# Delta-rule chain on block-diagonal 128x128 weights, modulation products in quarters, in a two-layer hybrid diffusion step

## The chip, the cores and the metric

The kernel runs on one core of a Trainium2 chip. The metric is the device time of one execution in microseconds (us), given as the median of several runs. TensorE is called PE in the rows, its weight load PEld; VectorE is DVE, ScalarE is ACT, GpSimd is POOL, and SP is the queue of SyncE, which issues the DMAs.

## The reference

One inference step of a backbone with two layers, on 128 context and 512 latent tokens of width 1024. Each layer has a mixer block with three branches (latent attention; gated linear attention; gated DeltaNet), whose results are projected, gated, summed and projected again, and then a SwiGLU block. Shift, scale and gate of both blocks come from a modulation. What the change touches is this:

```python
# modulation, per layer: six vectors of 1024 for the latent tokens, six for the context
mod = silu(cond) @ w_mod[l] + b_mod[l]
sh_a, sc_a, g_a, sh_f, sc_f, g_f = split(mod, 6)
...
h = h + g_a * y
...
# gated DeltaNet, 8 heads of 64, chunks of 64 tokens, both directions
def step(s, inp):
    u_n, w_n, qd_n, ke_n, a_n, ge_n = inp
    v_new = u_n - w_n @ s
    o_n = qd_n @ s + a_n @ v_new
    s = ge_n[..., None, None] * s + ke_n.T @ v_new
    return s, o_n
```

`u_n` and `w_n` are solutions of a triangular system of the chunk. All values are float32.

## The kernel before, in words

**Layout and large products.** Activations lie with channels on the 128 partitions and all 640 tokens in the free dimension. The large products (input projection, branch projections, output projection, SwiGLU) are one fixed sequence, an object `G` of class `Stream`. A weight tile of 128x512 is loaded (`wr`), rounded by ScalarE into `wh` (L465), and the rest is formed by GpSimd as `wl` (L466); each has three buffers. The activations are split in the same way (`xh`, `xl`; `oh`, `ol` for the branches). A block of 128x128 weights then gives six matmuls of 320 columns on L474: high by high, high by low, low by high, for two halves of the tokens. The result lies in a PSUM tile `gm` of the tag `g`, which has three buffers. When an output tile is done, a function posted for it reads it, such as `h_update` (L637), the residual update of the mixer's output projection `wo0` to `wo7`.

**Order.** Between the steps of the branches the program calls `fill(name)`, which emits as many steps of `G` as a table of numbers (`FILL`) gives for that place. A scheduler then orders the instructions of each engine by priorities and data; what stands in a queue at the end is fixed, and each engine works its queue in order. All the DMAs that are spoken of here are issued by SP, one after the other, and a DMA into a buffer that is still read waits there with all DMAs behind it.

**The chain.** `gdn_chain` (L924) works on one pair of heads `p` (four pairs per layer), on 10 chunks and in two directions: direction 0 runs forward, direction 1 backward. In a pair the two heads take the partitions 0 to 63 and 64 to 127. `steps` does one step of both directions:

- `k` times state (`ch<-S,bd_k`), then on VectorE `cy_` = that times a scale plus `v` (L947);
- `cy_` through the solved triangular matrix `t0` or `t1` (`ch<-cy_,bd_t`), then on VectorE the scaled copy `vs` (L959) and on ScalarE two copies to `VN` (L962), kept for the output;
- `kt` times `vs` (`ch<-vs,bd_kt`), and on VectorE the state's update (L973).

Each of these three products is done by `mm_heads` as two matmuls, with 64x64 weights and 64 columns, one per head. A layer has 224 such head pairs of products. Behind the steps of a pair come the output products: `pqs` (L996) with `bd_q`, whose 128x128 weights hold both heads on the diagonal and zeros elsewhere, and `pas` (L1001), then a norm and 128x128 transposes. `chain_load` loads the weights of the next pair, and the zeros of `bd_q` are written once per layer by two memsets (L1710).

**The modulation products.** In layer 0, the 20 rows 16 to 35 of the modulation weights, 16 to 23 of which are the mixer's gate, are multiplied beside the chain by `ModVe(bd, 4, 2)`: VectorE multiplies a weight tile `wmt` with the condition `cbb` and sums it up (L549, one step for latent and one for context, each with a read of the accumulator). The 1024 products of a row are split in two halves of 512 columns, `wmt` has four buffers, and a step is put behind every chain step; what is left over follows behind the chains in program order. Then the halves are summed (L555), and `mod_fix` adds the bias and scales the gate (L564, L570), which `h_update` reads. The rest of the rows is done later by steps of 1024 columns.

Of the kernel before, what the change touches and what calls it, by code (L numbers as in the profile page):

```python
# [9 lines left out]
F32 = mybir.dt.float32  # L10
# [8 lines left out]
P = 128  # L19
# [6 lines left out]
NCH = T // 64  # L26
# [257 lines left out]
class Stream:  # L284
    """Matrix products in a fixed order, emitted piece by piece between other work."""

# [86 lines left out]
def tile_hybrid(ctx: ExitStack, tc, a):  # L373
# [126 lines left out]

    # ---- modulation
    def mod_load(f, pool_):
# [19 lines left out]
    class ModVe:  # L522
        """Products of the condition with rows of the modulation weights, in single steps of the vector engine."""

# [57 lines left out]

    # ---- residual, norms
    HS = (slice(0, HF), slice(HF, T))
# [70 lines left out]
    def join(name, hs, nm, after, pre=None):  # L655
        """The last residual tile, the norm and its use, by halves of the tokens."""
        if pre:
            pre()
        G.to(name + "/0")
        G.steps(5)  # L660
        nm.fin(0)
        G.to(name)
        after(0, range(4))
        nm.fin(1)
        after(0, range(4, 8))
        after(1, range(8))

    # ---- DRAM scratch
    NB = [dp.tile([4, 2, NCH, 64, 64], F32, name=f"NB{d}") for d in range(2)]
# [6 lines left out]

    # ---- gated DeltaNet
    def gdn_gates(prm, misc, gp, X, fill):
# [141 lines left out]
    def turn_pairs(src, dst, scale):  # L820
        """Both heads of a pair from channels to tokens, chunk by chunk."""
        pv = psg("pvt").rearrange("p a (j c) -> p (a j) c", c=P)
        for j in range(5):
            pe.transpose(pv[:, j], src[:, j * P:(j + 1) * P], ident)
        for r in range(2):
            for h in range(2):
                se.activation(dst[h * 64:(h + 1) * 64, r::2], pv[r * 64:(r + 1) * 64, 0:5, h * 64:(h + 1) * 64], AF.Copy,
                              scale=scale)
# [6 lines left out]
    def gdn_solve(lp):  # L835
        Bb = lp.tile([P, 10, P], F32, name="Bb")
        ge.memset(Bb, 0.0)
        for d in range(2):
# [26 lines left out]
            for f in range(2):  # L865
                ln = slice(40 * f, 40 * f + 40)
                Lt = lp.tile([P, 10, 32], F32, name="Lt", tag="Lt")
                Rt = lp.tile([P, 10, 32], F32, name="Rt", tag="Rt")
                dma(Lt, LS[d][ln].rearrange("(g q) s c -> (q s) g c", q=4))
                for q in range(4):  # L870
                    qs = slice(32 * q, 32 * q + 32)
                    lq = slice(40 * f + q, 40 * f + 40, 4)
                    dma(Rt[qs], T3[lq, hi, hi].rearrange("g s c -> s g c"))
                    dma(Bb[qs, :, qs], N3[lq, lo, hi].rearrange("g s c -> s g c"))
                for _ in range(5):
                    yield
                def narrow(w):
                    """Bb[:, g].T @ w[:, g] for all g, by the narrow operand and a turn."""
                    pw = psb([P, 3, P], "pw")
                    for g in range(10):  # L880
                        r = slice(32 * (g % 4), 32 * (g % 4) + 32)
                        pe.matmul(pw[r, g // 4], w[:, g], Bb[:, g], start=True, stop=True)
                    wt = lp.tile([P, 3, P], F32, name="wt", tag="st")
                    se.activation(wt[:, 0:2], pw[:, 0:2], AF.Copy)
                    se.activation(wt[0:64, 2], pw[0:64, 2], AF.Copy)
                    yield
                    pt = psb([P, 3, P], "pt")
                    for i, n in ((0, P), (1, P), (2, 64)):
                        pe.transpose(pt[:, i, :n], wt[:n, i], ident[:n, :n])
                    return pt.rearrange("p i (r c) -> p (i r) c", c=32)[:, 0:10]  # L890

                pw = yield from narrow(Lt)
                for q in range(4):
                    qs = slice(32 * q, 32 * q + 32)
                    se.activation(Bb[qs, :, qs], pw[qs], AF.Copy)
                yield
                px = yield from narrow(Rt)
                xs = lp.tile([P, 10, 32], F32, name="xs", tag="Lt")
                se.activation(xs, px, AF.Copy)
                for q in range(4):  # L900
                    dma(T3[40 * f + q:40 * f + 40:4, lo, hi].rearrange("g s c -> s g c"), xs[32 * q:32 * q + 32])
                yield

    def chain_load(p, B, names):
        for n in names:
            if n in ("k", "kt"):
                dma(B[n], SPL[n][p])
                continue
            for h in range(2):
                hh = slice(h * 64, (h + 1) * 64)  # L910
                if n == "a":
                    for d in range(2):
                        dma(B[n][d * 64:(d + 1) * 64, h], SPL[f"a{d}"][p, hh])
                elif n == "q":
                    dma(B[n][hh, :, hh], SPL[n][p, hh])
                else:
                    dma(B[n][hh], TB[int(n[1])][p, h].rearrange("n s c -> s n c"))

    def mm_heads(out, w, x):
        for h in range(2):  # L920
            hh = slice(h * 64, (h + 1) * 64)
            pe.matmul(out[hh], w[hh], x[hh], start=True, stop=True)

    def gdn_chain(l, p, SC, B, kp, z, fill, mstep):  # L924
# [10 lines left out]
        def steps(sts):  # L935
            pss = [psb([P, 3, 64], "ch") for _ in sts]
            ys = []
            for (d, n, zero, dst), ps in zip(sts, pss):
                if not zero:
                    mm_heads(ps[:, 0], B["k"][:, n], S[:, n, d])  # L940
            for (d, n, zero, dst), ps in zip(sts, pss):
# [10 lines left out]
            for (d, n, zero, dst), ps, y in zip(sts, pss, ys):  # L952
                mm_heads(ps[:, 1], B[f"t{d}"][:, n], y)
            vss = []
# [11 lines left out]
            if vss:  # L966
                for (d, n, zero, dst), ps, vs in zip(sts, pss, vss):
                    mm_heads(ps[:, 2], B["kt"][:, n], vs)
                for (d, n, zero, dst), ps, vs in zip(sts, pss, vss):
# [58 lines left out]

    # ---- latent attention
    def latents(l, prm, misc, M, pj, gg, fill):  # L1030
# [223 lines left out]

    # ---- gated linear attention
    def gla(l, prm, misc, gp, oh, ol, gmf, gmb, fill, tick):
# [182 lines left out]

    # ---- the order of the large products  # L1440
    pieces = []
# [95 lines left out]

    # ---- the layers
    hctx = pool("hp0", "right")
# [35 lines left out]
    for l in range(L):  # L1575
# [107 lines left out]
        with pool("gt", "right", 2) as gt:  # L1683
# [11 lines left out]
            with pool("zs", "left") as zs:  # L1695
# [6 lines left out]
                with pool("bd", "left") as bd, pool("kp", "left") as kp:  # L1702
                    bufs = {}
                    bufs["a"] = bd.tile([P, 2, NCH, 64], F32, name="bd_a")
                    for n in ("t0", "t1", "k", "kt"):
                        bufs[n] = bd.tile([P, NCH, 64], F32, name="bd_" + n)
                    bufs["q"] = bd.tile([P, NCH, P], F32, name="bd_q")
                    mst = ModVe(bd, 4, 2).steps(0, range(16, 16 + OPT["mc"])) if l == 0 else iter(())
                    for h in range(2):
                        ge.memset(bufs["q"][h * 64:(h + 1) * 64, :, (1 - h) * 64:(2 - h) * 64], 0.0)  # L1710
                    chain_load(0, bufs, ("t0", "t1", "k", "kt"))
# [132 lines left out]
```

## Time and profile before

| | |
|---|---|
| median of 3 runs | 2895.55 us (2894.88 to 2895.70) |
| span of the profiled execution | 2896.0 us |
| PE busy | 2721.4 us (94%), 19444 instructions |
| PEld busy | 2498.5 us (86%) |
| DVE busy | 1542.6 us (53%) |
| ACT busy | 1209.0 us (42%) |
| POOL busy | 1196.0 us (41%) |
| DMA | 317.10 MB, mean 109 GB/s |
| L474 (three groups with `xh`, `xl`) | 846.2, 826.8, 832.5 us |
| L549 (all forms) | 298.6 us, 200 instructions |

Busy times can overlap: a matmul's record reaches from its start to its modelled end, so that records of neighbouring matmuls overlap, and the distance from start to start tells what one costs. A row of the timeline gathers neighbouring instructions of one kind (`x8`) and gives the start of the first and the time to the end of the last. Brackets at a row's end give the idle time ahead of it and who ended it.

### The profile page before, as it was taken

What the parts mean: (1) busy time and instruction counts of PE and PEld (TensorE: products, weight loads), DVE (VectorE), ACT (ScalarE), POOL (GpSimd) and SP (SyncE); (2) the same over time, 40 slices, a digit from 0 to 9 for tenths busy, and PEclk for the clock granted to TensorE, in tenths of its full rate; (3) what the DMA queues carried; (4) which work ended last, traced back from release to release, by engine and by line L of the source; (5) the groups of instructions that cost most, each with busy time, mean ns of one, the idle gap of its engine ahead of it and who ended that gap; (6) DMA issues with size and microseconds to landing.
All of it is one profiled execution on the core that took longest, in us unless ns stands there. A gap on an engine that the chain in (4) does not pass through costs nothing. (4 is left out here: it accounts for less than half of the span.)

```text
span 2896.0 us, 49763 instructions
## 1 busy us (share of the span) xinstructions
PE 2721.4 (94%) x19444; PEld 2498.5 (86%) x19444; DVE 1542.6 (53%) x2834; ACT 1209.0 (42%) x2276; POOL 1196.0 (41%) x872
## 2 busy tenths in 40 slices
PE   7899999889999999999998899987999999999998
PEld 4788888778779899999988888876877898999998
DVE  4765584747655699177358576556334334211212
ACT  5575655543333522122366645554333344222223
POOL 3543222333325467366445323233333264443443
PEclk9999999999999999999999999998999999999999
DMA  6254433245433355344323534332423231222222
GB/s 207 90 161 141 91 82 94 88 130 168 140 101 127 108 189 177 86 139 156 105 84 110 177 90 97 72 93 73 137 79 88 73 111 59 77 73 78 73 74 83
DMA packets 291834, 317.10 MB, mean 109 GB/s; under 512 B 163696, under 2 KB 174768, under 8 KB 291472
## 3 DMA queue, kind: packets, MB, share of 16 engines
q1 hardware_dynamic: 291600, 313.92, 37.3%
q8 instruction: 154, 2.52, 0.4%
q14 instruction: 80, 0.66, 0.1%
HBM read 266.01 MB, written 47.82 MB: 108 GB/s over the span
## 5 line engine op out<-in xcount | busy, mean ns | idle before, releaser
L466 POOL TENSOR_TENSOR wl<-wr,wh 128x512 fp32r<-128x512 f32 (+1 forms) x576 | 813.9, 1416 | 1307.0 <-ACT wh L465 1177.0
L474 PE MATMUL gm<-xh,wh 128*128 128x320 f32 x3456 | 846.2, 322 | 25.1 <-ACT xh L624 9.4
L474 PE MATMUL gm<-xh,wl 128*128 128x320 f32 x3456 | 826.8, 316 | 13.4 <-POOL wl L466 13.4
L474 PE MATMUL gm<-xl,wh 128*128 128x320 f32 x3456 | 832.5, 317 | 7.2 <-DVE xl L631 4.2
L465 ACT ACTIVATE wh<-wr 128x512 fp32r<-128x512 f32 (+1 forms) x576 | 357.6, 623 | 944.0 <-PE gm L474 648.9
L474 PEld LDWEIGHTS gm<-xh,wh 128*128 128x128 f32 x3456 | 589.6, 192 | 52.5 <-ACT xh L624 14.5
L474 PEld LDWEIGHTS gm<-xl,wh 128*128 128x128 f32 x3456 | 594.3, 192 | 25.0 <-DVE xl L631 9.8
L474 PEld LDWEIGHTS gm<-xh,wl 128*128 128x128 f32 x3456 | 592.6, 192 | 21.7 <-POOL wl L466 15.5
L549 DVE CUSTOM_DVE_ANT_0 ctb<-wmt,cbb 128x1024 f32<-128x1024 f32 (+1 forms) x200 | 298.6, 1493 | 3.4
L637 DVE SCALAR_TENSOR_TENSOR h<-gm,mod,h 128x128 f32<-128x128 f32 x144 | 55.7, 462 | 272.2 <-PE gm L474 266.1
L474 PE MATMUL gm<-ah,wh 128*128 128x320 f32 x704 | 164.6, 310 | 0.5 <-DVE h L637 0.5
L474 PE MATMUL gm<-ah,wl 128*128 128x320 f32 x704 | 164.1, 309 | 0.0
L474 PE MATMUL gm<-al,wh 128*128 128x320 f32 x704 | 163.9, 309 | 0.0
L962 ACT ACTIVATE VN<-ch 64x64 f32<-64x64 f32 x320 | 70.0, 219 | 178.5 <-DVE vs L959 164.5
L474 PEld LDWEIGHTS gm<-ah,wh 128*128 128x128 f32 x704 | 118.7, 188 | 1.6 <-DVE h L637 1.5
L474 PEld LDWEIGHTS gm<-al,wh 128*128 128x128 f32 x704 | 118.5, 188 | 0.2
L474 PEld LDWEIGHTS gm<-ah,wl 128*128 128x128 f32 x704 | 118.5, 188 | 0.0
L1773 DVE TENSOR_TENSOR th<-th,gm 128x640 f32<-128x640 f32 x44 | 36.2, 822 | 149.2 <-PE gm L474 148.4
L1766 DVE SCALAR_TENSOR_TENSOR th<-th,gm 128x640 f32<-128x640 f32 x44 | 35.9, 816 | 138.3 <-ACT th L1765 138.3
L479 POOL TENSOR_TENSOR al<-th,ah 128x640 fp32r<-128x640 f32 x44 | 89.5, 2033 | 28.0 <-DVE ah L478 28.0
L474 PE MATMUL gm<-ol,wh 128*128 128x320 f32 x384 | 99.3, 332 | 1.5 <-POOL ol L479 1.5
L474 PE MATMUL gm<-oh,wh 128*128 128x320 f32 x384 | 98.7, 334 | 0.5 <-DVE gth L1524 0.3
(747 smaller groups left out, 3822.8 us busy)
## 6 DMA issues: line engine op xcount, KB each, us to landing
wr<-in_wall_dram SPq DMA_DIRECT2D x432, 256.0 KB, 3.0
wmt<-in_wmodt_dram SPq DMA_DIRECT2D x60, 512.0 KB, 3.7
wr<-in_wfo_dram SPq DMA_DIRECT2D x64, 256.0 KB, 2.6
wr<-in_wbr_dram SPq DMA_DIRECT2D x48, 256.0 KB, 2.7
wmt<-in_wmodt_dram SPq DMA_DIRECT2D x40, 256.0 KB, 3.2
wm<-in_wmod_dram SPq DMA_DIRECT2D x16, 512.0 KB, 8.3
wr<-in_wfo_dram SPq DMA_DIRECT2D x32, 192.0 KB, 2.4
h<-in_xt_dram SPq DMA_DIRECT2D x16, 320.0 KB, 5.5
```

The source lines that it names most:

```text
L465: se.activation(wh[:, :w], wr[:, :w], AF.Copy)
L466: ge.tensor_tensor(wl[:, :w], wr[:, :w], wh[:, :w], op=ALU.subtract)
L474: pe.matmul(ps[:, c, :HF], w_[:, wsl], x_[kx][:, c * HF:(c + 1) * HF], start=(start and i == 0), stop=(stop and i == 2))
L479: (lo or ge).tensor_tensor(dst_l, src, dst_h, op=ALU.subtract)
L549: ins = ve.tensor_tensor_reduce(self.t, wm, self.c[:, i], 0.5, 0.0, ALU.mult, ALU.add, accum_out=acc[h][:, m - m0, i:i + 1])
L637: ve.scalar_tensor_tensor(hs[d][:, s:e], ps[:, c, s - c * HF:e - c * HF], g[:, d, i:i + 1], hs[d][:, s:e], op0=ALU.mult, op1=ALU.add)
L962: se.activation(VN[d * 64:(d + 1) * 64, h, n], ps[h * 64:(h + 1) * 64, 1], AF.Copy)
L1766: ve.scalar_tensor_tensor(v3(th), v3(th), 1.0, ps, op0=ALU.add, op1=ALU.mult)
L1773: ve.tensor_tensor(v3(th), v3(th), ps, op=ALU.mult)
```

## The change

The weights of the three chain products become block-diagonal 128x128, as `bd_q` has been: `t0`, `t1`, `kt` and `k` get 128 columns per chunk, each head's 64x64 block is loaded onto the diagonal, and the rest is zeroed once per layer by two memsets per buffer (ten memsets instead of two). One matmul of 64 columns then serves both heads, and `mm_heads` goes. `k` and `kt` are loaded in two DMAs of 64 partitions each instead of one of 128. `ModVe` is made with two buffers and four quarters: steps of 256 columns. Further lines of the diff only remove comments, which shifts line numbers by 8 behind the chain.

```diff
 def chain_load(p, B, names):
     for n in names:
-            if n in ("k", "kt"):
-                dma(B[n], SPL[n][p])
-                continue
             for h in range(2):
                 hh = slice(h * 64, (h + 1) * 64)
                 if n == "a":
...
-                elif n == "q":
+                elif n in ("q", "k", "kt"):
                     dma(B[n][hh, :, hh], SPL[n][p, hh])
                 else:
-                    dma(B[n][hh], TB[int(n[1])][p, h].rearrange("n s c -> s n c"))
-
-    def mm_heads(out, w, x):
-        for h in range(2):
-            hh = slice(h * 64, (h + 1) * 64)
-            pe.matmul(out[hh], w[hh], x[hh], start=True, stop=True)
+                    dma(B[n][hh, :, hh], TB[int(n[1])][p, h].rearrange("n s c -> s n c"))
...
-                    mm_heads(ps[:, 0], B["k"][:, n], S[:, n, d])
+                    pe.matmul(ps[:, 0], B["k"][:, n], S[:, n, d], start=True, stop=True)
...
-                mm_heads(ps[:, 1], B[f"t{d}"][:, n], y)
+                pe.matmul(ps[:, 1], B[f"t{d}"][:, n], y, start=True, stop=True)
...
-                    mm_heads(ps[:, 2], B["kt"][:, n], vs)
+                    pe.matmul(ps[:, 2], B["kt"][:, n], vs, start=True, stop=True)
...
-                    for n in ("t0", "t1", "k", "kt"):
-                        bufs[n] = bd.tile([P, NCH, 64], F32, name="bd_" + n)
-                    bufs["q"] = bd.tile([P, NCH, P], F32, name="bd_q")
-                    mst = ModVe(bd, 4, 2).steps(0, range(16, 16 + OPT["mc"])) if l == 0 else iter(())
-                    for h in range(2):
-                        ge.memset(bufs["q"][h * 64:(h + 1) * 64, :, (1 - h) * 64:(2 - h) * 64], 0.0)
+                    for n in ("t0", "t1", "kt", "k", "q"):
+                        bufs[n] = bd.tile([P, NCH, P], F32, name="bd_" + n)
+                    mst = ModVe(bd, 2, 4).steps(0, range(16, 16 + OPT["mc"])) if l == 0 else iter(())
+                    for n in ("t0", "t1", "kt", "k", "q"):
+                        for h in range(2):
+                            ge.memset(bufs[n][h * 64:(h + 1) * 64, :, (1 - h) * 64:(2 - h) * 64], 0.0)
```

What the scheduler makes of it is seen in three places. The first is TensorE in the chain of layer 1, before, with two matmuls (x2) per head pair:

```order
L922 MATMUL ch<-vs,bd_kt 64x64 x2
L474 MATMUL gm<-xh,wl 128x320
L922 MATMUL ch<-vs,bd_kt 64x64 x2
L474 MATMUL gm<-xh,wh 128x320 x2
L922 MATMUL ch<-S,bd_k 64x64 x2
L474 MATMUL gm<-xl,wh 128x320
L922 MATMUL ch<-S,bd_k 64x64 x2
L474 MATMUL gm<-xl,wh 128x320
L474 MATMUL gm<-xh,wl 128x320 x2
L922 MATMUL ch<-cy__21764,bd_t_20741 64x64 x2
```

and a stretch of the same chain in the changed kernel:

```order
L474 MATMUL gm<-xl,wh 128x320
L474 MATMUL gm<-xh,wl 128x320 x2
L474 MATMUL gm<-xh,wh 128x320 x2
L960 MATMUL ch<-vs,bd_kt 128x64
L932 MATMUL ch<-S,bd_k 128x64
L474 MATMUL gm<-xl,wh 128x320 x2
L474 MATMUL gm<-xh,wl 128x320
L932 MATMUL ch<-S,bd_k 128x64
L474 MATMUL gm<-xh,wl 128x320
L945 MATMUL ch<-cy__22786,bd_t_20707 128x64
```

Each `x2` has become one matmul, and chain products still stand singly or in twos between stream matmuls.

The second is VectorE at the last modulation steps of layer 0. Before, they stand in the output of the third pair of heads (`co`, `css`, L1008 to L1016), ahead of the chain of the fourth:

```order
L549 ISA ctb,macc_6408<-wmt,cbb 128x512
L549 ISA macc_6408 128x1
L555 TENSOR_TENSOR mod_102<-mod_102,macc_6408 128x40
L1012 TENSOR_REDUCE css<-co_8298 128x10
L564 TENSOR_TENSOR mod_102<-mod_102,prm_162 128x16 x2
L570 TENSOR_SCALAR mod_102<-mod_102 128x16
L1016 TENSOR_TENSOR co<-co,css 128x640
```

In the changed kernel the last ones stand right ahead of the residual updates of `wo0` to `wo2` (`h_9475` to `h_9477`), behind 30 more of their kind:

```order
L549 ISA ctb,macc_6416<-wmt,cbb 128x256
L549 ISA macc_6416 128x1
L549 ISA ctb,macc_6416<-wmt,cbb 128x256
L549 ISA macc_6416 128x1
L555 TENSOR_TENSOR mod_102<-mod_102,macc_6416 128x40
L564 TENSOR_TENSOR mod_102<-mod_102,prm_162 128x16 x2
L570 TENSOR_SCALAR mod_102<-mod_102 128x16
L637 SCALAR_TENSOR_TENSOR h_9475<-gm,mod_102,h_9475 128x128
L637 SCALAR_TENSOR_TENSOR h_9475<-gm,mod_102,h_9475 128x192
L637 SCALAR_TENSOR_TENSOR h_9475<-gm,mod_102,h_9475 128x320
L637 SCALAR_TENSOR_TENSOR h_9476<-gm,mod_102,h_9476 128x128
```

The modulation's end has moved behind all four chains and the merge of the third branch.

The third is the queue of SP where it loads the projection weights of the third branch (`wr<-in_wbr_dram`), before:

```order
L389 DMA wr<-in_wall_dram 128x512
L389 DMA wr<-in_wbr_dram 128x512 x7
L389 DMA wr<-in_wall_dram 128x512 x5
L389 DMA cbb<-in_condb_dram 128x2048
L389 DMA h_9509<-in_xt_dram 128x640
```

and in the changed kernel:

```order
L389 DMA wr<-in_wbr_dram 128x512
L389 DMA wmt<-in_wmodt_dram 128x256 x8
L389 DMA wr<-in_wbr_dram 128x512
L389 DMA wmt<-in_wmodt_dram 128x256 x2
L389 DMA wr<-in_wbr_dram 128x512
L389 DMA wmt<-in_wmodt_dram 128x256 x3
L389 DMA wr<-in_wbr_dram 128x512 x2
L389 DMA wmt<-in_wmodt_dram 128x256 x3
L389 DMA wr<-in_wall_dram 128x512
```

Loads of modulation weights now stand between the loads of the stream.

## Rows read from the trace of the kernel before

**Rows 1.** Windows: busy us (instructions) per engine, clock, DMA share; chains of layers 0, 1.

```profile
644.20:875.70 231.50, 228.06 (x1935) 182.16 (x1936) 149.70 (x454) 80.35 (x229) 74.70 (x59) 0.99 0.48 137
2079.50:2303.00 223.50, 219.92 (x1912) 176.91 (x1913) 85.78 (x286) 77.61 (x223) 69.58 (x59) 0.98 0.32 88
```

**Rows 2.** Windows, the same stretches, line L474 alone (PE, PEld).

```profile
644.20:875.70 231.50, 166.13 (x825) 124.69 (x825) 0.99 0.48 137
2079.50:2303.00 223.50, 165.14 (x816) 123.00 (x816) 0.98 0.32 88
```

**Rows 3.** Timeline of PE from 695 us: start, duration, engine, line, operation, tiles.

```profile
695.06 0.46 PE L474 MATMUL gm<-xl,wh 128*128 128x320 f32 x2
...
695.64 0.46 PE L474 MATMUL gm<-xh,wh 128*128 128x320 f32 x2
```

**Rows 4.** Windows, both chains together, line L1001 (`pas`) alone.

```profile
sum 455.00, PE 9.51 PEld 8.07; mean PE 4.75 PEld 4.04
```

**Rows 5.** Timeline of PE, chain of layer 0, around one isolated product.

```profile
712.77 0.31 PE L474 MATMUL gm<-oh,wl 128*128 128x320 f32 x1
713.01 0.33 PE L922 MATMUL ch<-vs,bd_kt 64*64 64x64 f32 x4
713.27 0.41 PE L474 MATMUL gm<-oh,wl 128*128 128x320 f32 x1
713.52 0.31 PE L474 MATMUL gm<-oh,wh 128*128 128x320 f32 x1
```

**Rows 6.** Timeline of PE, chain of layer 1, first and next `k` products of a step.

```profile
2278.26 0.45 PE L922 MATMUL ch<-S,bd_k 64*64 64x64 f32 x8
...
2282.72 0.45 PE L922 MATMUL ch<-S,bd_k 64*64 64x64 f32 x8
```

**Rows 7.** Timeline of PE, start of the kernel.

```profile
20.76 1.05 PE L519 MATMUL pmt<-C_base,mr 128*128 128x2 f32 x8 [0.80 <-DVE mr L516]
```

**Rows 8.** Timeline of PE, other 128x128 weights within the stream.

```profile
603.08 0.46 PE L474 MATMUL gm<-xh,wl 128*128 128x320 f32 x2
603.37 0.60 PE L1370 MATMUL pu<-gvt,ez 128*128 128x128 f32 x4
...
604.11 0.31 PE L474 MATMUL gm<-xl,wh 128*128 128x320 f32 x1
```

**Rows 9.** Timelines of PE, DVE and ACT, one step of pair 3, layer 0.

```profile
851.59 0.33 PE L922 MATMUL ch<-S,bd_k 64*64 64x64 f32 x4
...
852.94 0.33 PE L922 MATMUL ch<-cy__8669,bd_t 64*64 64x64 f32 x4
...
854.59 0.33 PE L922 MATMUL ch<-vs,bd_kt 64*64 64x64 f32 x4
...
855.94 0.33 PE L922 MATMUL ch<-S,bd_k 64*64 64x64 f32 x4
...
851.97 0.29 DVE L947 SCALAR_TENSOR_TENSOR cy__8669<-ch,SC,cvt 128x64 f32<-128x64 f32 x1 [0.41 <-PE ch L922]
...
855.02 0.28 DVE L973 SCALAR_TENSOR_TENSOR S<-S,GE,ch 128x64 f32<-128x64 f32 x1 [0.81 <-PE ch L922]
...
853.64 0.45 ACT L962 ACTIVATE VN<-ch 64x64 f32<-64x64 f32 x2 [3.44 <-DVE vs L959]
```

**Rows 10.** Groups by line, DVE, 640 to 880 us: busy us, mean ns | idle.

```profile
L549 DVE CUSTOM_DVE_ANT_0 ctb<-wmt,cbb 128x512 f32<-128x512 f32 x80 | 69.1, 864 | 0.3
```

**Rows 11.** Timeline of DVE: last modulation read; residual update of the second output tile.

```profile
826.02 0.08 DVE L549 DVE_READ_ACCUMULATOR2_ANT macc<- 128x1 f32 x1
...
929.72 1.13 DVE L637 SCALAR_TENSOR_TENSOR h<-gm,mod,h 128x128 f32<-128x128 f32 x3 [3.16 <-PE gm L474]
```

**Rows 12.** Tile `wmt`, its loads on SP: ns min/median/max, first and last start.

```profile
L389 SPq DMA_DIRECT2D wmt<-in_wmodt_dram x100: 327/328/1861, 641.7 to 1368.3; - x100
```

**Rows 13.** DMA issues, 600 to 940 us: KB each, median us to landing.

```profile
wmt<-in_wmodt_dram SPq DMA_DIRECT2D x40, 256.0 KB, 3.2
```

**Rows 14.** Tile `bd_q`, its memsets on POOL: ns min/median/max.

```profile
L1710 POOL MEMSET bd_q<- x4: 626/626/626, 623.4 to 2059.6; 64x640 f32 x4
```

## The prediction, made before the changed kernel ran

> **What bounds the kernel now.** The change touches two stretches, the delta-rule chains of layer 0 (644 to 876 us) and of layer 1 (2080 to 2303 us), so I read these first, by engine: TensorE is busy 228.06 of 231.50 us and 219.92 of 223.50 us, VectorE 149.70 and 85.78 [rows 1]. So a chain is paid in TensorE time, as long as its products never wait. Next I asked what TensorE does there. 825 and 816 of its records are stream matmuls of 320 columns [rows 2]. Undisturbed they start every 0.1465 us (four in 0.586 us [rows 3]): 120.9 and 119.5 us. The 40 query products are 80 records of about 0.11 us, the price of a full-weight record in [rows 7, 8]: 8.8 us. The `pas` products have 9.51 us in both windows together [rows 4], 4.8 each. What is left, 97 and 90 us, belongs to the 224 chain products of a layer (two heads each), with some waits and 15 transposes (about 2 us): about 95 and 88 us, or 0.42 and 0.39 us per product. That is far more than the arithmetic: two products back to back end 0.45 us after their start, one 0.33 us [rows 5, 6], so a dense one adds 0.12 us.
>
> The timeline tells why. Three stream matmuls with one chain product among them start at 712.77, 713.27 and 713.52: two intervals of 0.1465 us would be 0.29 us, but they took 0.75 us. The isolated product costs 0.46 us [rows 5]. Both edges are slow: 0.24 us before its first record, 0.26 us to the next stream matmul, and 0.25 us instead of 0.15 us behind that one. Where both directions stand together, a step has 18 stream matmuls and six products in 4.46 us [rows 6]: (4.46 - 2.64) / 6 = 0.30 us each. The reader is to see that the cost lies at the border between 64x64 and 128x128 weights, not in the product.
>
> **The change, part by part.** *Chain products.* Each of 224 head pairs per layer becomes one product with 128x128 weights and 64 columns, in two passes. No row shows that shape, so I bound a pass by its neighbours: with 2 columns eight passes are counted in 1.05 us with the last one's drain [rows 7], 0.112 us from start to start; with 128 columns, four passes put between stream matmuls lengthen 603.08 to 604.11 from 4 x 0.1465 = 0.59 to 1.03 us [rows 8], 0.11 us each, slow restart included. 64 columns lie between, so a product costs 2 x 0.112 = 0.224 us wherever it stands: 50 us per layer. Ceiling of the gain: 95 - 50 = 45 and 88 - 50 = 38 us. Floor: by the printed order, before, 120 (layer 0) and 100 (layer 1) products stand alone, 27 and 56 times two stand together. Alone saves 0.46 - 0.224 = 0.23 us, together 0.08 us each, dense ones nothing: 28 + 4 = 32 and 23 + 9 = 32 us. I take the ceiling, because it holds everything that was measured in the windows, and put the waits that replace it in a term of their own.
>
> [...]
>
> *New waits in the chain.* One step of pair 3 in layer 0 takes 4.35 us (851.59 to 855.94) with 11 stream matmuls [rows 9]. With cheap products it would take 11 x 0.1465 + 6 x 0.224 = 2.96 us. The dependent loop, from the same rows: state product to `cy_` 0.4 + 0.28 us, solve product at 852.94 to the end of its `VN` copies at 854.09, 1.15 us, update product at 854.59 to the end of `S` at 855.30, 0.71 us; with hand-overs 2.7 us. That fits, with 0.3 us to spare, so part of the gain turns into waits. Bounds: nothing, and the whole gain. For layer 1 I take 10 us: 32 steps at 0.3 us. Layer 0 also has the modulation steps on VectorE ahead of chain operations; before, 80 of them (mean 0.864 us [rows 10]) sat there without waiting for a load. Now they are half as long, but have two buffers instead of four, and one that waits for its load holds the chain's `cy_`, `vs` and `S` behind it. I take 17 us: the 10 and 27 steps at 0.25 us. Chains in all: -45 - 38 + 10 + 17 = -56 us.
>
> *Modulation products in quarters.* 160 steps of 256 columns replace 80 of 512, with an accumulator read of 0.08 us each [rows 11]. In the printed order 94 of the 160 stand ahead of the last chain product of layer 0, 16 up to the merge of branch 2, 18 in it, and the last 32 right ahead of the first residual update, which reads their result. Before, the last one ended at 826 us, more than 100 us ahead of the second tile's update at 929.72 [rows 11]. So 66 steps, 33 weight tiles, are new work between chain and update. The buffer ring sets a floor: issue 0.33, landing 3.2 us [rows 12, 13], two steps of about 0.55 us (half of 0.864, the read, some contention) make 4.6 us per buffer, with two buffers 2.3 us per tile: 76 us. TensorE has cover from 875.5 to the end of the third output tile: the second one's update starts at 929.72, released by TensorE, the third is 48 x 0.1465 = 7.0 us later, 61 us. Then its three PSUM buffers are full and it waits. 76 - 61 = 15 us; I take 14. Bounds: 0 (VectorE's other work overlaps the loads) and 30 us. Late next is the end of the norm, which moves with it.
>
> *Memsets and loads.* Eight more memsets per layer, 0.626 us each on GpSimd [rows 14], 5.0 us ahead of the splits `wl` and `ol`. Whether a split is late for TensorE by that I cannot read, so I take 1.5 us per layer, between 0 and 5. `k` and `kt` come in two loads of 256-byte pieces, as `bd_t` does already, and at least 96 stream matmuls, 14 us, stand in the printed order between the last product of a pair and the first of the next: nothing. Without that cover it would be about a landing per pair, 3.2 us by the larger pieces of [rows 13].
>
> Sum: -56 + 14 + 3 = -39 us against the profiled span of 2896.0 us, which is 0.45 us above the median of the runs: **2857 us**.
>
> **The rivals.**
> *The chain becomes bound by its latency.* Its loop needs 2.7 us even with free products; if hand-overs on VectorE stretch it to 3.7 us per step, half of the gain goes. For it: the loop is nearly as long as the new TensorE work. Against: in layer 1 many steps carry 12 or 18 stream matmuls. 32 us of gain are left, less 17: 2881 us.
>
> *The ring of two starves the layer's end (slower than before).* Place: merge of branch 2 and output projection of layer 0. If the sync queue holds the second load behind a stream load that waits for GpSimd, the two buffers no longer overlap and a tile costs 4.6 us: 33 x 4.6 = 152 us against 61, a stall of 91 us, 2896 - 56 + 91 + 3 = 2934 us. It decides from (61 + 53) / 33 = 3.5 us per tile. For it: in the new order eight such loads stand between two stream loads. Against: a stall gives the queue nothing else to wait for.
>
> *Dense rates hold everywhere.* If the border costs the same with 128x128 weights, only the dense price changes: 448 x (0.224 - 0.12) = +47 us, with 17 us beside it 2960 us. Against it stands the run in [rows 8]: full weights of another product go in and out of the stream at their dense price.
>
> **How the numbers follow.** Forecast 77%, latency 12%, starved ring 8%, dense rates 3%. Uncertain within the forecast are the chain gain (floor 64, ceiling 83 us), the waits (0 to 40), the stall (0 to 30) and the memsets (0 to 10). The ceiling with 13 us of waits and no stall or memset gives 2826 us; the floor with 27 us of waits, a stall of 24 and 3 us of memsets gives 2886 us. This range also holds the latency case; it leaves out the other two rivals and a tenth of the forecast. About 0.2%, 5.8 us, can be told from no change. Faster: forecast but for the end of its tail, and latency, 86%; same, that end, 3%; slower, the starved ring and the dense rates, 11%.
>
> **What would show it.** Chain windows near 200 and 193 us; a product between stream matmuls adding 0.22 us; no slow restart after it; four of them in a step waiting for `VN` or `S`. In layer 0 the first residual update starts 70 us or more behind the last chain product, with TensorE idle before the fourth output tile. Wrong would be: chain windows that shrink by less than 15 us each, a stall over 40 us at the output projection, or pieces of the stream waiting for `wr`.

## The result, and the profile after

The changed kernel took 2911.93 us (median of 4 runs, 2909.13 to 2916.99), the kernel before beside it 2895.22 us: ratio 1.0071, 95% interval 1.0053 to 1.0088. It is slower by 17 us where 39 us of gain were forecast, and outside the range. Its profiled span is 2912.3 us, 16.3 us longer than before. The page's first part, busy time of each engine, shows less work on PE than the table ahead (2721.4 us), and more on VectorE (1542.6):

```profile
PE 2699.5 (93%) x18548; PEld 2543.7 (87%) x18548; DVE 1579.3 (54%) x3000; ACT 1208.3 (41%) x2280; POOL 1199.3 (41%) x888
```

So 22 us less of PE's time went with 16 us more of the whole.

Both kernels issue the same 13824 stream matmuls (L474), so the start of the n-th one in both traces gives a lag, and differences of lags give what a stage cost. All stages below are cut at the same five matmuls, one profiled execution for each kernel (before, they start at 635.3, 890.0, 1025.9, 2076.4 and 2341.6 us):

| stage | forecast | measured |
|---|---|---|
| up to layer 0's chain | 0 | +1.8 |
| chain of layer 0 and the turn behind it | -45 + 17 = -28 | -9.0 |
| merge, output projection, norm of layer 0 | +14 | +35.4 |
| from there to the chain of layer 1 (its memsets) | +3, both layers | +4.2 |
| chain of layer 1 | -38 + 10 = -28 | -16.0 |
| rest | 0 | -0.2 |

In all the runs below, the first of these stages, whose work no edit changes, lies between -0.7 and +5.7 us. A difference of a few us in one stage of one profile therefore shows nothing by itself.

First the windows of the changed kernel, PE alone: stretch, length, busy (instructions), granted clock, DMA share, GB/s, for the chain of layer 0, the end of layer 0, and the chain of layer 1:

```profile
647.10:869.70 222.60, 211.14 (x1499) 0.95 0.45 121
875.00:1050.00 175.00, 141.31 (x827) 0.87 0.40 130
2111.00:2319.40 208.40, 201.77 (x1467) 0.96 0.36 90
```

and of the kernel before, the end of layer 0 (its chains are in [rows 1]):

```profile
875.00:1025.00 150.00, 140.96 (x926) 0.95 0.39 126
```

TensorE was busy in all but 3.4 and 3.6 us of the chains before; now it is idle 11.5 and 6.6 us. And the granted clock, which was 0.99 and 0.98 in the chains [rows 1], is lower in all three. Short windows show two levels of it, 1.00 (changed kernel, 773.5 to 775 us) and 0.50 (777 to 782 us), and at the low one stream matmuls start every 0.27 us (two in 0.54, 780.28 to 780.82 us), against 0.1465 at the high one [rows 3], less than twice as long. So 1 minus the mean, times the length, bounds the time lost: 11.1 + 22.8 + 8.3 = 42 us after, 2.3 + 7.5 + 4.5 = 14 us before. Part of that fell in idle time, in which TensorE ran nothing. Half of the time in which TensorE was busy at the low level is 10.2 + 15.5 + 8.5 = 34 us after and 3.2 + 5.6 + 3.3 = 12 us before. So the clock explains at most 22 of the miss of 55 us, and the prediction had no term for it. At least 33 us are something else, above all waits.

**The product costs what was forecast.** Timeline of PE, changed kernel, one chain product among stream matmuls of layer 1, against [rows 5]:

```profile
2241.06 0.30 PE L474 MATMUL gm<-xh,wh 128*128 128x320 f32 x1
2241.20 0.33 PE L945 MATMUL ch<-cy__22144,bd_t 128*128 128x64 f32 x2
2241.34 0.39 PE L474 MATMUL gm<-xh,wh 128*128 128x320 f32 x1
2241.58 0.45 PE L474 MATMUL gm<-xl,wh 128*128 128x320 f32 x2
```

From 2241.06 to 2241.58 it is 0.52 us, two intervals of 0.1465 us less: 0.23 us, where such a place cost 0.46 us before. That is the price where nothing is awaited: the two records of a `kt` product mostly start 0.16 us apart, those of the others 0.06, so that a `kt` costs 0.1 us more. Experiment e4 tells why.

**Short waits, and the clock behind them.** Where a pair begins, products follow one another with little or nothing between, and the stream can be late as well. Timeline of PE at the second and the third pair of layer 0, a wait for `VN` and one for `wl`:

```profile
711.55 0.91 PE L960 MATMUL ch<-vs,bd_kt 128*128 128x64 f32 x4 [0.80 <-ACT VN L954]
...
775.25 0.56 PE L474 MATMUL gm<-xh,wl 128*128 128x320 f32 x2 [1.69 <-POOL wl L466]
```

and the windows around the second of these waits:

```profile
773.00:773.50 0.50, 0.50 (x5) 1.00 0.00 0
773.50:775.00 1.50, 0.07 (x1) 1.00 0.00 0
775.00:776.00 1.00, 0.75 (x5) 1.00 0.00 0
776.00:783.00 7.00, 7.00 (x33) 0.51 0.49 152
783.00:784.00 1.00, 1.00 (x9) 1.00 0.29 64
```

A wait of 1.69 us is followed by 7 us at a granted clock of 0.51, although TensorE is busy in all of them: up to 3.4 us more. Each of the eight low stretches in the two chains of the changed kernel begins behind an idle time of 0.6 to 1.7 us; not each such idle time is followed by one (1.34 us at 696 us was not). So the order in time is shown, and not what makes the difference.

**The end of layer 0.** Waits of PE from 870 to 1000 us (total, times, longest):

```profile
PE gm L474 <- DVE h L637: 14.4, 2, 14.2
PE gm L474 <- ACT wh L465: 3.5, 1, 3.5
PE gm L474 <- POOL xl L1521: 2.5, 2, 1.3
PE gm L474 <- DVE oh L478: 2.4, 1, 2.4
PE gm L474 <- DVE gth L1516: 2.4, 1, 2.4
```

The tile `wmt` from 870 to 962 us (ns min/median/max, first and last start; then VectorE's idle time for it):

```profile
L549 DVE CUSTOM_DVE_ANT_0 ctb<-wmt,cbb x66: 408/425/1839, 870.8 to 960.2; 128x256 f32<-128x256 f32 x66
L389 SPq DMA_DIRECT2D wmt<-in_wmodt_dram x35: 327/328/552, 872.2 to 956.5; - x35
...
  DMA wmt<-in_wmodt_dram: 16.3, 13
```

66 steps were forecast behind the chain, and there are 66; they end 91 us behind the last chain product (869.7), 76 were forecast; before, the last one ended at 826 us [rows 11]. The fourth output tile then waits 14.2 us; 14 was the forecast. The agreement is luck: the steps end 15 us later than forecast, but TensorE also comes to this tile 78.5 us behind the last chain product (at 948.2 us), and not 61. Before that, it waited in small pieces that were not counted, for `wh` (its load, issued at 937.60 us, stood behind loads of `wmt` and `h` that the sync queue issued from 926.57 us on), for `oh`, `gth` and `xl`. And the clock: windows of PE in the wait, behind it, and behind the norm:

```profile
948.20:962.70 14.50, 0.30 (x3) 0.69 0.65 217
962.70:967.50 4.80, 4.79 (x19) 0.53 0.00 0
...
1004.50:1022.00 17.50, 14.97 (x46) 0.51 0.06 15
```

### The profile page after: what moved, and what is told of

Read it like the earlier page. It is cut to its first block, busy times and chain, and to the rows that moved or that the text cites. A ratio compares the mean times of both kernels' runs of the same rounds, so it can differ in the third digit from the quotient of the medians.

```text
span 2912.3 us, 48150 instructions
## 1 busy us (share of the span) xinstructions
PE 2699.5 (93%) x18548; PEld 2543.7 (87%) x18548; DVE 1579.3 (54%) x3000; ACT 1208.3 (41%) x2280; POOL 1199.3 (41%) x888
## 5 line engine op out<-in xcount | busy, mean ns | idle before, releaser
L474 PE MATMUL gm<-xh,wh 128*128 128x320 f32 x3456 | 848.8, 323 | 47.0 <-DVE h L637 14.7
L474 PE MATMUL gm<-xl,wh 128*128 128x320 f32 x3456 | 838.6, 319 | 11.1 <-DVE xl L631 5.8
L474 PE MATMUL gm<-xh,wl 128*128 128x320 f32 x3456 | 832.7, 318 | 12.7 <-POOL wl L466 12.7
L474 PEld LDWEIGHTS gm<-xh,wh 128*128 128x128 f32 x3456 | 596.2, 194 | 68.1 <-issue 25.2
L474 PEld LDWEIGHTS gm<-xl,wh 128*128 128x128 f32 x3456 | 599.2, 194 | 23.6 <-DVE xl L631 11.1
L474 PEld LDWEIGHTS gm<-xh,wl 128*128 128x128 f32 x3456 | 598.4, 193 | 17.1 <-POOL wl L466 15.4
L549 DVE CUSTOM_DVE_ANT_0 ctb<-wmt,cbb 128x256 f32<-128x256 f32 (+1 forms) x280 | 321.5, 1148 | 22.2 <-DMA wmt<-in_wmodt_dram 17.1
L474 PE MATMUL gm<-ah,wh 128*128 128x320 f32 x704 | 164.6, 310 | 0.5 <-DVE h L637 0.5
L474 PE MATMUL gm<-ah,wl 128*128 128x320 f32 x704 | 164.1, 309 | 0.0
L474 PE MATMUL gm<-al,wh 128*128 128x320 f32 x704 | 163.9, 309 | 0.0
L474 PEld LDWEIGHTS gm<-ah,wh 128*128 128x128 f32 x704 | 118.7, 188 | 1.6 <-DVE h L637 1.5
L474 PEld LDWEIGHTS gm<-al,wh 128*128 128x128 f32 x704 | 118.5, 188 | 0.2
L474 PEld LDWEIGHTS gm<-ah,wl 128*128 128x128 f32 x704 | 118.6, 188 | 0.0
L474 PE MATMUL gm<-oh,wl 128*128 128x320 f32 x384 | 96.9, 331 | 5.7 <-POOL wl L466 5.7
L474 PE MATMUL gm<-oh,wh 128*128 128x320 f32 x384 | 99.2, 337 | 2.7 <-DVE oh L478 2.4
```

The costliest lines, as they stand in the source:

```text
L474: pe.matmul(ps[:, c, :HF], w_[:, wsl], x_[kx][:, c * HF:(c + 1) * HF], start=(start and i == 0), stop=(stop and i == 2))
L549: ins = ve.tensor_tensor_reduce(self.t, wm, self.c[:, i], 0.5, 0.0, ALU.mult, ALU.add, accum_out=acc[h][:, m - m0, i:i + 1])
```

## The experiments

Theory M: the modulation steps, put behind the chains by a ring of two, cost the end of the layer. Theory W: the chain loses its gain to waits, above all of `kt` for ScalarE's copies `VN`. Lags of stages below are taken as in the table above, against the kernel before.

**e1: only the quarters.** In the kernel before:

```diff
-                    mst = ModVe(bd, 4, 2).steps(...)
+                    mst = ModVe(bd, 2, 4).steps(...)
```

> The kernel before with its chain of 64x64 weights kept, and only the modulation products changed: quarters with two buffers. In the trace of the changed kernel TensorE leads by 7 us at the last chain product of layer 0 and lags by 27 us when the fourth output tile starts; after that nothing is won back until the chain of layer 1. Theory M (the modulation steps, deferred behind the chains and waiting in a ring of two, cost this end of the layer some 34 us): slower than before by 25 to 35 us, 2920 to 2930 us, with a wait of TensorE of over 8 us for the first residual update. Rival C (the end is late because of the chain on full weights: its outputs, its clock, its memsets): within 5 us of before, 2890 to 2900 us.

2919.93 us, ratio 1.0090 (1.0075 to 1.0105): M, not C. The long wait for the first residual update did not come, though: the end of the layer cost 18.3 us in smaller waits, and the chain of layer 0 7.1 us, with a granted clock of 0.82 from 650 to 700 us. The quarters alone cost 26 us; the whole change costs 17, so that its chain part, in both layers, wins only some 9 if the two parts add up.

**e2: fewer rows beside the chain.** In the changed kernel:

```diff
-    'mc': 20
+    'mc': 12
```

> The changed kernel with 12 instead of 20 modulation rows beside the chain (96 quarter steps instead of 160); the other 8 rows join the later steps of 1024 columns beside the output projection. In the printed order 87 of the 96 steps now stand ahead of the last state update of layer 0 and only 9 between it and the first residual update. Theory M: the stall goes, and 16 more steps of 1.2 us beside the output projection cost at most 8 us: 2877 to 2888 us, faster than before. Rival C: 2905 to 2915 us.

2891.48 us, ratio 0.9991 (0.9978 to 1.0004): 20 us better than the changed kernel, but short of the range. The chain of layer 0 gained 17.0 us, 8 more than in the changed kernel, though nothing in its products or copies was edited; the end still cost 22.1, as the rows only moved. Waits of PE there, 860 to 985 us:

```profile
PE gm L474 <- DVE h L637: 8.5, 1, 8.5
PE gm L474 <- ACT wh L465: 3.6, 1, 3.6
```

**e3: the new chain in layer 1 alone.** The kernel before, where `l == 1` gets the block-diagonal buffers, loads, memsets and single matmuls:

```diff
     def mm_heads(out, w, x):
+        if w.shape[-1] == P:
+            pe.matmul(out, w, x, start=True, stop=True)
+            return
...
```

> The kernel before with block-diagonal weights in the chain of layer 1 alone; layer 0 and its modulation products as before (halves, four buffers). From the traces the chain of layer 1 won 12 us where 28 were forecast. If that is the chain's own gain: 2881 to 2887 us, faster than before by 8 to 15 us, with dips of the granted clock in the chain again. Rival (the small gain in layer 1 is an after-effect of the late layer 0, whose loads and clock it inherits): the forecast 28 us, 2865 to 2870 us.

2884.11 us, ratio 0.9966 (0.9954 to 0.9978), 10 us faster than before: the small gain is the chain's own. Its stage won 18.3 us in the profiled run, where 28 were forecast, and 5.7 were lost ahead of both chains, where nothing was edited.

**e4: `VN` not read from PSUM.** In the changed kernel (the outputs of the chain then leave out the scale):

```diff
-                    se.activation(VN[...], ps[h * 64:(h + 1) * 64, 1], AF.Copy)
+                    se.activation(VN[...], ps[h * 64:(h + 1) * 64, 1] if dst is None else vs[h * 64:(h + 1) * 64], AF.Copy)
```

> The changed kernel with the copies VN taken from vs in SBUF instead of from the PSUM tile (so VN holds the scaled values and the outputs of the chain leave that scale out). Then the product kt x vs needs no copy of ScalarE to have ended. Theory W (the weight load of kt waits for ScalarE's copies, which shows as 0.40 us for an isolated kt product against 0.31 us for k and t, and as waits up to 0.8 us): layer 1's chain is 5 to 12 us shorter than in the changed kernel, and its kt products cost 0.31 us like the others. Rival P (it is the price of this product, or of the PSUM bank): the chain of layer 1 changes by under 3 us. The whole time also carries the modulation's deferral (79 instead of 68 steps behind the last state update): 2895 to 2910 us by W, 2912 to 2920 us by P.

2901.72 us, ratio 1.0032 (1.0015 to 1.0048), and the chain stages -17.8 and -27.9 us: 9 and 12 us better than in the changed kernel. Groups of PE in the chain of layer 1 (busy, mean ns | idle before), changed kernel:

```profile
L960 PE MATMUL ch<-vs,bd_kt 128*128 128x64 f32 x144 | 30.4, 295 | 4.4 <-ACT VN L954 4.0
L932 PE MATMUL ch<-S,bd_k 128*128 128x64 f32 x144 | 25.0, 267 | 0.1
```

and e4:

```profile
L961 PE MATMUL ch<-vs,bd_kt 128*128 128x64 f32 x144 | 23.3, 262 | 2.3 <-DVE vs L951 2.3
L932 PE MATMUL ch<-S,bd_k 128*128 128x64 f32 x144 | 23.3, 264 | 0.4 <-DVE S L964 0.2
```

W in layer 1: without ScalarE's reads the records of `kt` fall from 295 to 262 ns, like those of `k`, which is 4.8 us for 144 of them; the time lost at the low clock falls by another 5 us (mean granted clock 0.98, and 0.96 in the changed kernel). The chain of layer 1 then has its forecast gain of 28 us. In layer 0 the 9 us do not show W: e2 and e8 leave both copies as they are, `kt` still waits 2.3 and 2.9 us for `VN` there (3.4 in the changed kernel), and the stage wins 17.0 and 18.6 us. `kt` writes another column of the PSUM tile that ScalarE is still reading, and it waits all the same: 4.0 us in the chain of layer 1 of the changed kernel (`<-ACT VN` in its row above). What would come of not waiting no run here shows.

**e5: one copy by VectorE first.** In e3, for both layers:

```diff
+                    u = kp.tile([P, 64], F32, name="vu", tag="vu", bufs=2)
+                    ve.tensor_copy(u, ps[:, 1])
-                    ve.tensor_scalar(vs, ps[:, 1], SC[...], None, op0=ALU.mult)
+                    ve.tensor_scalar(vs, u, SC[...], None, op0=ALU.mult)
...
-                    se.activation(VN[...], ps[h * 64:(h + 1) * 64, 1], AF.Copy)
+                    se.activation(VN[...], ps[h * 64:(h + 1) * 64, 1] if dst is None else u[h * 64:(h + 1) * 64], AF.Copy)
```

> The kernel of e3_layer1_only (block-diagonal weights in layer 1 alone), with the products of the solve copied once by VectorE from PSUM to SBUF; vs and the copies VN are both made from that copy, so nothing is left out, and kt x vs no longer waits for ScalarE. VectorE gets one more operation of about 0.28 us per direction and step. Theory W (e4 took 10 us more out of the chain of layer 1): the chain of layer 1 is 5 to 10 us shorter than in e3 and the whole 2874 to 2880 us. Rival: the copy is itself a link in front of vs, 0.3 us in each of some 18 steps of a pair, and gives it all back: 2882 to 2888 us.

2896.50 us, ratio 1.0001 (0.9987 to 1.0014): the rival, and worse. In the profiled run layer 1's chain won 10.9 us, 7 less than in e3; the other loss, 11.7 us, lies in the old chain of layer 0, which has the extra copy too. Now `kt` waits for VectorE, chain of layer 1:

```profile
L922 PE MATMUL ch<-vs,bd_kt 128*128 128x64 f32 x144 | 27.8, 292 | 10.1 <-DVE vs L965 10.1
```

**e6: a ring of five.** In the changed kernel:

```diff
-        vt = kp.tile([P, NCH, 64], F32, name="cvt", tag="cvt")
+        vt = vn(z)
...
-                    mst = ModVe(bd, 2, 4).steps(...)
+                    mst = ModVe(bd, 5, 4).steps(...)
```

> The changed kernel with v loaded into the (then unused) tile z of the pair, which frees 2.5 KB per partition, and five instead of two buffers for the quarters of modulation weights. In the printed order 129 instead of 92 of the 160 steps stand ahead of the last state update of layer 0, 31 behind it, and the last of these 16 rows of VectorE ahead of the first residual update. Theory M with the ring as its cause: the stall of 14 us goes and the end of the layer costs under 12 us instead of 31: 2885 to 2895 us. Rival Q (not the ring, but 160 short steps with their reads as such are too much for VectorE): 2903 to 2915 us.

2888.06 us, ratio 0.9980 (0.9971 to 0.9990). The same 160 steps, tile `wmt` from 640 to 905 us:

```profile
L549 DVE CUSTOM_DVE_ANT_0 ctb<-wmt,cbb x160: 406/418/1793, 653.2 to 902.7; 128x256 f32<-128x256 f32 x160
...
  DMA wmt<-in_wmodt_dram: 0.2, 1
```

end at 902.7 instead of 960.2 us, hardly wait for a load (last line), the stall is gone, and the end of the layer costs 8.7 instead of 35.4 us. So it is the ring, and not the short steps as such: M.

**e7: a ring of four and e5's copy.** In the changed kernel, with e6's `vt = vn(z)`:

```diff
-                    mst = ModVe(bd, 2, 4).steps(...)
+                    mst = ModVe(bd, 4, 4).steps(...)
...
+                    ve.tensor_copy(u, ps[:, 1])
```

> Both in the changed kernel: v in the tile z with a ring of four for the quarters, and the early copy of the solved product (vs and VN from SBUF). 120 of 160 modulation steps ahead of the last state update of layer 0. If the two causes add up: e6 less 10 to 20 us for the two chains, 2868 to 2882 us, faster than both kernels. Rival: VectorE, which has the modulation steps and one more copy per step, becomes the bound of layer 0's chain: chain of layer 0 over 222 us, 2888 us or more.

2901.23 us, ratio 1.0020 (1.0009 to 1.0031). The rival's time, and its sign too: layer 0's chain won 4.9 of its 231.5 us, so it is over 222. But VectorE's modulation steps are not the whole of it: the chain of layer 1, which has none beside it, won only 7.5 us, and `kt` waits 7.5 us there for `vs`, behind the copy, as in e5.

**e8: the gate's rows first.** In the changed kernel:

```diff
+    def two_groups(m):
+        yield from m.steps(0, range(16, 24))
+        yield from m.steps(0, range(24, 16 + OPT["mc"]))
...
-                    mst = ModVe(bd, 2, 4).steps(...)
+                    mst = two_groups(ModVe(bd, 2, 4))
```

> The changed kernel, ring of two, with the 8 rows of the mixer's gate as a group of their own ahead of the other 12 rows. The first residual update then needs only the first group, which ends within the chain. The same number of steps, the same loads (and four more small loads of the condition). If the 14 us are the update's wait for its gate: that wait goes, but 41 quarter steps move beside the output projection, where VectorE is the busier engine (in e2 it cost 19 us there): 2892 to 2905 us. Rival (the order of loads on the sync queue is what holds TensorE at the layer's end): 2908 to 2915 us, with waits for wh or wl over 8 us.

2912.12 us, ratio 1.0060 (1.0045 to 1.0075): no gain, the rival's time, with 6.7 us of waits for `wh` and `wl` where it asked for 8. The wait for the update has gone, as meant, and another stands in its place, PE, 870 to 1000 us:

```profile
PE cs L611 <- DVE nacc L602: 7.0, 1, 7.0
PE gm L474 <- ACT wh L465: 5.0, 2, 4.3
```

with the end of the layer at +40.1 us, while its chain won 18.6. All steps must end before the norm is used, whichever tile waits first, so the lateness of the last step is paid in either order. The prediction's "late next is the end of the norm" was right and should have been priced.

**e9: ring of four, one copy by ScalarE.** In the changed kernel, with `vt = vn(z)`:

```diff
+                u = ps[:, 1]
+                if dst is not None:
+                    u = kp.tile([P, 64], F32, name="vu", tag="vu", bufs=2)
+                    se.activation(u, ps[:, 1], AF.Copy)
                 for h in range(2):
-                    se.activation(VN[...], ps[h * 64:(h + 1) * 64, 1], AF.Copy)
+                    se.activation(VN[...], u[h * 64:(h + 1) * 64], AF.Copy)
```

> The changed kernel with v in the tile z, a ring of four for the quarters, and the solved product copied from PSUM once by ScalarE, in one operation over all 128 partitions beside VectorE's vs; the two copies VN are made from that copy, behind it. kt x vs then waits for one copy of ScalarE instead of two, and VectorE gets nothing more to do (in e5 and e7 its extra copy cost more than it gave). Theory W (the two copies on ScalarE are the late link): against e6 each layer's chain loses 3 to 8 us: 2873 to 2884 us. Rival V (what made e4 quick was that ScalarE did not read that PSUM tile at all, so any copy from it holds kt): 2886 to 2893 us, with kt still waiting for ScalarE.

2882.52 us, ratio 0.9959 (0.9945 to 0.9973): W by the whole time, but not in each layer. Against e6, layer 0's chain gained 9 us (-17.4), that of layer 1 only 1.5 (-16.2), where 3 to 8 were asked; the end of layer 0 is at +11.5. The wait for two copies is gone, `kt` in layer 1:

```profile
L964 PE MATMUL ch<-vs,bd_kt 128*128 128x64 f32 x144 | 27.2, 275 | 0.7 <-ACT vu L956 0.6
```

The clock took the gain back (0.50 from 2144.5 to 2154 and from 2202.5 to 2212 us), each time behind 2.4 us of idle time at the start of a pair. Timelines of DVE and PE at the first of these:

```profile
2142.09 0.82 DVE L1520 SCALAR_TENSOR_TENSOR gth<-gth,gm 128x640 f32<-128x640 f32 x1 [9.29 <-PE gm L474]
2142.83 2.68 DVE L1023 TENSOR_TENSOR z<-ptr,z 64x192 f32<-64x192 f32 x8
...
2144.39 0.66 PE L945 MATMUL ch<-z,bd_t 128*128 128x64 f32 x2 [2.40 <-issue]
```

The row names no releaser, but the kernel does: `ch` and the transposed outputs `ptr` of the pair before share two PSUM buffers (tag `b`). The fourth of VectorE's eight reads of `ptr`, the last of the first buffer, ends at 2144.29, and the weights of the pair's first product are loaded from 2144.36; the eighth ends at 2145.52, and those of the other direction's follow at 2145.59. The distance of 0.07 us is the same at the two starts in e6 and the two in e12. In the changed kernel VectorE did these reads 8.6 us ahead of `gth`; with `v` in the tile `z`, they come behind it. So the room for the ring has a price in layer 1.

**e10 and e11: e9's copy by ScalarE in e3, and then an even fill table for layer 1** (three of its fifteen new numbers):

```diff
-    'steps1_1@1': 1.72, 'steps2_1@1': 0.0, 'steps3_1@1': 0.66
+    'steps1_1@1': 0.82, 'steps2_1@1': 1.23, 'steps3_1@1': 0.82
```

> The kernel of e3_layer1_only with the same single copy by ScalarE (both layers). W: the chain of layer 1 3 to 8 us shorter than in e3, the whole 2875 to 2882 us. V: 2883 to 2889 us.

> The kernel of e10 with other numbers in the fill table for layer 1: the same stream work, but evenly over the three places of a chain step with most behind the solve product (0.82, 1.23, 0.82 in pairs 1 to 3, before for instance 1.72, 0, 0.66). Theory T (the chain waits because the table was set for products twice as dear, so stream work stands where nothing is awaited): the waits of kt, k and the solve product and the dips of the clock get fewer, 3 to 8 us less than e10. Rival S (the scheduler orders TensorE by its own estimate, and the table moves little): within 3 us of e10.

2888.08 us (2881.12 to 2917.52) and 2887.05 us (2879.55 to 2917.60), ratios 0.9991 (0.9963 to 1.0019) and 1.0002 (0.9969 to 1.0035): no verdict for either theory, since the old chain of layer 0 spoils both (+27.5 and +36.0 us in the profiled runs). Layer 1's chain stands at -15.3 (e10) and -19.8 us (e11), where e3 has -18.3: one profile each, against W and for T, and too little to decide. Windows of PE in it, e10:

```profile
800.00:806.00 6.00, 5.54 (x49) 1.00 0.50 171
806.00:832.00 26.00, 26.00 (x161) 0.54 0.40 107
```

and before:

```profile
806.00:832.00 26.00, 25.64 (x230) 1.00 0.64 165
```

**e12: the memsets on VectorE**, in e9. In the changed kernel, POOL ahead of the chain of layer 1:

```profile
2095.25 0.86 POOL L1702 MEMSET bd_q<- 64x640 f32 x1
2096.09 3.10 POOL L479 TENSOR_TENSOR ol<-z,oh 128x640 fp32r<-128x640 f32 x2
2099.24 0.86 POOL L1702 MEMSET bd_q<- 64x640 f32 x1
2100.19 1.53 POOL L479 TENSOR_TENSOR ol<-z,oh 128x640 fp32r<-128x640 f32 x1
2101.67 1.26 POOL L466 TENSOR_TENSOR wl<-wr,wh 128x512 fp32r<-128x512 f32 x1
```

and PE:

```profile
2102.99 0.56 PE L474 MATMUL gm<-oh,wl 128*128 128x320 f32 x2 [3.89 <-POOL wl L466]
```

```diff
-                            ge.memset(bufs[n][...], 0.0)
+                            ve.memset(bufs[n][...], 0.0)
```

> The kernel of e9_ring4_scalar_copy with all ten memsets of a layer on VectorE instead of GpSimd. In the changed kernel GpSimd works on eight memsets of 0.6 us and the splits ol in turn just ahead of the chain of layer 1; the first wl behind them is late, TensorE waits 3.9 us for it and its clock falls for the next 4 us (before: 0.8 us at this place, and a fall as well). Theory Z (the memsets cost their own time on GpSimd, 4 to 6 us in layer 1): the wait of 3.9 us goes and the time falls by 2 to 6 us against e9: 2876 to 2881 us. Rival (GpSimd's splits ol would be as late without them, or VectorE is now late with oh): 2881 to 2886 us, with a wait of over 2 us for wl or oh at the same place.

2874.23 us, ratio 0.9928 (0.9911 to 0.9946): more than Z asked for, 8 us less than e9, and the wait of 3.9 us is gone (the longest idle time left there is 1.6 us, at the first chain product). The kernel before has no wait for `wl` at this place; the 0.8 us of the expectation are one of `kt` for `VN`, at 2080 us. The last 150 stream matmuls ahead of layer 1's chain take 22.5 us before, 28.2 in the changed kernel, 28.3 in e9 and 22.5 in e12, so the memsets cost 5.7 us here. e12 beats both kernels, the changed one by 38 us.

## Why the prediction was wrong, point by point

- *Price of a product, 0.224 us*: right, 0.23 us measured where nothing is awaited. The dense-rates rival fell: between stream matmuls a product with 64x64 weights cost 0.46 us [rows 5], where the prediction's dense price was 0.12 [rows 5, 6], and with 128x128 weights it costs 0.23.
- *Chain gain 45 + 38 us less waits 17 + 10*: the step that failed in the chains is the term of the waits. Measured are -9.0 and -16.0 us, so 36 and 22 us of the gain were lost to waits and clock; layer 0's window shrank by 8.9 us, which is the prediction's own sign of being wrong (under 15). In layer 1, e4 gives -27.9 us by taking ScalarE's reads away, so these copies and the low clock behind them are the 12 us that were missing there. In layer 0, 19 us were missing; TensorE is idle 8 us more there than before and loses 7 us more to the clock, but as e2 and e8 win 8 and 10 us more than the changed kernel with the copies in place, the cause there stays open. The prediction had seen the copies (1.15 us from solve product to `VN`) and still priced waits by the mean of a step, 2.96 against 2.7 us, as if stream matmuls stood just where something is awaited. At the starts of pairs they don't. The latency rival, given 12%, had the size of the chains' gain nearly right (32 us, 25 measured), but not the link: in layer 1 it is ScalarE's copies, and not hand-overs on VectorE.
- *Stall of 14 us before the fourth output tile*: right in place; that 14.2 us were measured is luck, as two errors cancel (steps 15 us later, cover 17 us longer). *End of the layer as a whole*: wrong by 21 us, the second term that failed. At most 10 us of that are the clock (15.5 us lost while busy against 5.6), the rest are small waits ahead of the stall. The mechanism of the starved ring, given 8%, is the right one in kind (slower, and at this place), but not in size: a tile took about 91 / 33 = 2.8 us, not 4.6. e6 shows that it is the ring: with five buffers the end costs 8.7 us.
- *Memsets 1.5 us per layer*: too small in layer 1, where they cost 5.7 us (3.89 us of wait for `wl`, and a low clock behind it); e12 won 8 us by moving them in both layers, so the bound of 5 was too low for layer 1.
- *No clock term*: put at nothing without a reason, and worth up to 22 of the 55 us. Each wait was priced by its own length; the trace shows 7 us at half clock behind 1.69 us of waiting. Our reading is that the slow borders had kept TensorE occupied, and that taking this work out of a chain nearly bound by its latency left short idle times. The traces show more idle time and a lower clock (idle 11.5 and 6.6 us in the two chains, 3.4 and 3.6 before; clock 0.95 and 0.96, 0.99 and 0.98 before). But idle time alone does not account for the clock: in e1 the old chain of layer 0 lost 7 us more to it with only 1.3 us more idle time. What brings the clock down stays open.

## What to carry over

Where a change makes TensorE's part of a dependent chain cheaper, compare the chain's links with the work between them place by place, at the starts above all, and price a new wait by its length and by the low clock that can follow it (7 us at 0.51 behind 1.69 us here). Space that a change takes from a ring of loads is a term like any other: with two buffers the steps came 57 us later than with five. And a wait that was only moved (e2, e8) came back at the next place (the end of layer 0 still cost 22.1 and 40.1 us); look for what must end before the next common point.

## What the runs showed that was not expected

The old chain of 64x64 weights can lose its clock too: with one more copy on ScalarE (e10) TensorE ran 26 us on end at 0.54 with no record of a wait over 0.33 us ahead of it, and single runs of this kernel lie between 2881 and 2918 us; those of e9, with full weights in both layers, lie between 2881 and 2884. Why some runs of e10 escape it is open. Open too is what slows layer 0's chain in the changed kernel and not in e2 and e8, and whether a fill table made for the new prices would win more.
